# HGRN forget gates and queries by seven products for two heads, with frame operands made once

## The chip, the cores and the metric

The kernel runs on one core of a Trainium2 chip. The metric is the device time of one execution in microseconds (us); a profiled execution also records every engine's instructions, and its span is the time from the first to the last of them.

## What is computed

One layer of a streaming encoder on x of 512 frames by 1024 channels, all in float32. One input projection gives eight parts: zu and zv for a gMLP branch, zq, zf, zi and zo for an HGRN2 recurrence with 8 heads of 128 channels, and two merge gates.

```python
h = rmsnorm(x, norm_mix[l])
proj = h @ w_in[l]
zu, zv, zq, zf, zi, zo, g_a, g_b = jnp.split(proj, split_points, axis=-1)
y_a = gmlp_branch(zu, zv, gmlp_ln_g[l], gmlp_ln_b[l], gmlp_ws[l], gmlp_bs[l]) @ w_up_a[l]
y_b = hgrn2_branch(zq, zf, zi, zo, lower_bounds[l], l, hg_norm_g[l]) @ w_up_b[l]
mix = jax.nn.sigmoid(g_a) * y_a + jax.nn.sigmoid(g_b) * y_b
x = x + mix @ w_out[l]
h = rmsnorm(x, norm_ffn[l])
x = x + jnp.square(jax.nn.relu(h @ w_ff1[l])) @ w_ff2[l]
```

In the recurrence the forget gate is sigmoid(zf), the key k = sigmoid(-zf), the query q = silu(zq); per head S_t = diag(f_t) S_(t-1) + k_t v_t^T and o_t = S_t^T q_t. Each head's o is normalised and gated with silu(zo).

## The kernel before

Every product of float32 matrices is made of reduced-precision matmuls: `split` (L97 to L99) makes a high part H by a copy on ACT (L98) and a low part L by a subtraction on DVE (L99), and `mm3` (L122 to L124) issues three matmuls, H·H, H·L and L·H, for each block of 128 input channels. Weights come in tiles of 128 x 1024 (512 KB) by `wraw` on the queue of SP (L94), four raw tiles in flight; `operand` splits them into WH and WL, of which there are five. `hTH` and `hTL` hold the normalised frames, channels on partitions.

There are two ways to project. `chan_proj` multiplies one weight tile with all 512 frames: 8 blocks x 3 = 24 matmuls of 512 columns for 128 channels. `seven` computes two such tiles at once in a Strassen-Winograd form: the weights of two tiles A and B are seen as 2 x 2 blocks (two groups of 128 channels, two halves of the input channels), the frames as 2 x 2 blocks (two halves of the input channels, two halves of the frames), and seven block products of 12 matmuls of 256 columns replace eight. The sums of weight blocks (s1 to s4) are made on DVE (L147, L148, L154, L155) before they are split; the sums of frame blocks (t1, t2, t4) are made and split once by `frames_operands`.

The stages in order: the norm of x and its transposition; zv and zu with the gMLP branch, whose result y is split into `yaH` and `yaL` group by group (L367); four rounds of the recurrence; the output gate zo (L556 to L559); the projection upa of the gMLP branch (L571); the merge gates GA and GB by `seven`, with `frames_operands` just ahead of them (L593); upb, the output projection, and the two products of the feed-forward part (FFN), of which the first uses four plain tiles and then `seven` with its own frame operands (L675). The last 24 tiles of the FFN's second product add weight tiles with accumulating transfers on the queue of POOL (L760).

A round takes two heads. `proj_round` makes V for both, then for each head forget gate F and key K out of one `chan_proj`, and query Q out of another (Q is gated on DVE, L405). `hgrn_head` has many small matmuls: cell products `sp` of 32 to 96 columns (L417), each followed by masks and decay products on DVE that change K and Q in place; at the end the transposes `pk` of K, the states `pst`, and the output `po` (L534, L536), which is squared on ACT (L538), turned into a factor on POOL (L216, L218) and scaled into `o_n` on DVE (L541).

The program is written stage by stage. A scheduler with a timeline simulation (`schedule_with_timeline_sim=True`) sets the order of the instructions on each engine, so that the projections of the next round lie between the heads of this one; each engine then runs its list in order.

Of the kernel before, what the change touches and what calls it, by code (L numbers as in the profile page):

```python
# [75 lines left out]
def trunk_kernel(ctx: ExitStack, tc: tile.TileContext, A: dict, out: bass.AP):  # L76
# [91 lines left out]
    def frames_operands(pool, H, L, tmp):
# [12 lines left out]
        t1, t2, t3, t4 = x["11"], x["22"], x["12"], x["21"]
        nc.vector.tensor_tensor(t1, x["12"], x["11"], ALU.subtract)
        split(t1, *out["t1"])
        nc.vector.tensor_tensor(t3, x["22"], x["12"], ALU.subtract)
        nc.vector.tensor_tensor(t2, x["22"], t1, ALU.subtract)
        split(t2, *out["t2"])
        split(t3, *out["t3"])
        nc.vector.tensor_tensor(t4, x["21"], t2, ALU.subtract)
        split(t4, *out["t4"])
# [720 lines left out]
```

## Time and profile before

| what | value |
|---|---|
| median of 3 runs | 835.21 us (834.03 to 835.6) |
| profiled execution | 836.09 us, its span 834.2 us |
| mean granted TensorE clock | 0.993 |
| PE busy | 818.7 us, 98%, 6226 instructions |
| PEld (weight loads, beside PE) | 730.5 us, 88% |
| DVE busy | 599.2 us, 72% |
| ACT busy | 408.5 us, 49% |
| POOL busy | 47.1 us, 6% |

Shares are of the span. Matmuls overlap each other, so the time between the starts of two neighbours, and not the listed duration, is what one costs. The granted clock is a share of 2.4 GHz.

### The profile page before, as it was taken

The numbers are of one execution on the slowest core, as the hardware profiler recorded it, in microseconds if no ns is written. First come the engines' busy times: TensorE is split into PE (matmuls) and PEld (weight loads), VectorE is DVE, ScalarE is ACT, GpSimd is POOL, SyncE is SP. The second block draws the span as 40 slices with busy tenths as digits, with TensorE's granted clock in tenths as the row PEclk, the third lists the DMA queues.
The fourth block names the chain that finished last, engine by engine and source line by source line (L and its number), as shares of the span: only waits on it lengthen the run. The fifth ranks groups of instructions, "written<-read, shape, count | busy, mean of one in ns | idle before, by whom it ended". The sixth has DMA issues, their size and how long they took to land.

```text
span 834.2 us, 15111 instructions
## 1 busy us (share of the span) xinstructions
PE 818.7 (98%) x6226; PEld 730.5 (88%) x6226; DVE 599.2 (72%) x955; ACT 408.5 (49%) x676; POOL 47.1 (6%) x81
## 2 busy tenths in 40 slices
PE   8999999999999999999999999899999999999996
PEld 7989888879789988999878889899999988878884
DVE  7563767676685587887574369777777575899996
ACT  6433434344333345556442343677677652555454
POOL 2000000000000000000000021000000000010103
PEclk9999999999999999999999999899999999999998
DMA  9233321221311212323434411233333396193802
GB/s 337 88 110 106 98 67 68 73 66 40 102 52 52 93 36 76 102 101 103 152 101 173 156 62 41 77 105 120 105 103 101 104 303 176 43 292 99 235 11 101
DMA packets 26919, 92.44 MB, mean 111 GB/s; under 512 B 3489, under 2 KB 3873, under 8 KB 26850
## 3 DMA queue, kind: packets, MB, share of 16 engines
q1 hardware_dynamic: 24546, 84.13, 30.4%
q0 software_dynamic: 1728, 6.29, 4.1%
q8 instruction: 49, 0.80, 0.4%
q10 hardware_dynamic: 576, 1.05, 0.3%
q14 instruction: 20, 0.16, 0.1%
HBM read 89.36 MB, written 2.10 MB: 110 GB/s over the span
## 4 chain that ended last, share of the span: by engine, by line
PE 94%; DVE 2%; ACT 1%; issue 1%; POOL 1%; POOLq 0%; ACTq 0%; DVEq 0%
PE acc L122 15%; PE acc L124 15%; PE acc L123 15%; PE prodx L124 5%; PE prodx L122 5%; PE prodx L123 5%; PE prodzy L123 4%; PE prodzy L124 4%; PE prodzy L122 4%; PE hm L122 3%; PE hm L124 3%; PE hm L123 3%; PE y L122 2%; PE y L124 2%; PE y L123 2%; PE sp L417 2%
## 5 line engine op out<-in xcount | busy, mean ns | idle before, releaser
L99 DVE TENSOR_TENSOR WL<-raw,WH 128x1024 fp32r<-128x1024 f32 (+1 forms) x134 | 151.4, 1134 | 101.4 <-ACT WH L98 100.5
L98 ACT ACTIVATE WH<-raw 128x1024 fp32r<-128x1024 f32 (+1 forms) x134 | 132.2, 989 | 164.6 <-PE acc L123 62.7
L122 PE MATMUL acc<-WH,hTH 128*128 128x256 f32 x320 | 91.5, 286 | 0.0
L124 PE MATMUL acc<-WH,hTL 128*128 128x256 f32 x320 | 91.3, 285 | 0.0
L123 PE MATMUL acc<-WL,hTH 128*128 128x256 f32 x320 | 91.0, 284 | 0.0
L122 PE MATMUL acc<-hTH,WH 128*128 128x512 f32 x160 | 64.2, 401 | 0.0
L124 PE MATMUL acc<-hTH,WL 128*128 128x512 f32 x160 | 64.2, 401 | 0.0
L123 PE MATMUL acc<-hTL,WH 128*128 128x512 f32 x160 | 63.5, 397 | 0.0
L99 DVE TENSOR_TENSOR WL<-s,WH 128x1024 fp32r<-128x1024 f32 x44 | 53.8, 1222 | 10.0 <-ACT WH L98 9.0
L122 PEld LDWEIGHTS acc<-WH,hTH 128*128 128x128 f32 x320 | 60.3, 189 | 0.6
L123 PEld LDWEIGHTS acc<-WL,hTH 128*128 128x128 f32 x320 | 60.3, 188 | 0.5
L124 PEld LDWEIGHTS acc<-WH,hTL 128*128 128x128 f32 x320 | 60.3, 189 | 0.2
L98 ACT ACTIVATE WH<-s 128x1024 fp32r<-128x1024 f32 x44 | 46.7, 1062 | 16.1 <-PE prodx L123 9.5
L123 PE MATMUL hm<-WL,aH 128*128 128x512 f32 x96 | 38.0, 396 | 0.0
L124 PE MATMUL hm<-WH,aL 128*128 128x512 f32 x96 | 38.0, 395 | 0.0
L122 PE MATMUL hm<-WH,aH 128*128 128x512 f32 x96 | 37.9, 396 | 0.0
L124 PEld LDWEIGHTS acc<-hTH,WL 128*128 128x128 f32 x160 | 30.0, 188 | 7.1
L123 PEld LDWEIGHTS acc<-hTL,WH 128*128 128x128 f32 x160 | 30.0, 188 | 6.6
L122 PEld LDWEIGHTS acc<-hTH,WH 128*128 128x128 f32 x160 | 30.0, 188 | 6.5
L98 ACT ACTIVATE WH<-rawx 128x1024 fp32r<-128x1024 f32 x24 | 25.1, 1054 | 19.6 <-issue 10.7
L122 PE MATMUL prodx<-h2H,WH 128*128 128x256 f32 x112 | 31.4, 280 | 1.8 <-ACT WH L98 1.8
L123 PE MATMUL prodzy<-h2L,WH 128*128 128x256 f32 x112 | 32.1, 287 | 0.0
(295 smaller groups left out, 2344.6 us busy)
## 6 DMA issues: line engine op xcount, KB each, us to landing
raw<-in_w_dram SPq DMA_DIRECT2D x128, 512.0 KB, 3.6
rawx<-in_w_dram SPq DMA_DIRECT2D x18, 512.0 KB, 8.5
rawx<-in_w_dram POOLq DMA_DIRECT2D x6, 512.0 KB, 6.6
raw<-in_w_dram POOLq DMA_DIRECT2D x6, 512.0 KB, 8.1
x_t<-in_x_dram SPq DMA_DIRECT2D x4, 512.0 KB, 5.7
x<-in_x_dram SPq DMA_DIRECT2D x4, 512.0 KB, 5.2
out_dram<-x ACTq DMA_DIRECT2D x4, 256.0 KB, 2.8
out_dram<-x SPq DMA_DIRECT2D x4, 256.0 KB, 2.4
```

What stands on the lines that cost most here:

```text
L98: nc.scalar.activation(H, src, AF.Copy)
L99: nc.vector.tensor_tensor(L, src, H.bitcast(F32), ALU.subtract)
L122: nc.tensor.matmul(acc, ah, bh, start=first and i == 0, stop=False, **kw)
L123: nc.tensor.matmul(acc, ah, bl, start=False, stop=False, **kw)
L124: nc.tensor.matmul(acc, al, bh, start=False, stop=last and i == n - 1, **kw)
L417: nc.tensor.matmul(sp[p * C:(p + 1) * C, t * n:(t + 1) * n], K[:, t * P + p * C:t * P + (p + 1) * C], x(t, p), start=True, stop=True)
```

## The change

The forget gates and keys of both heads of a round now come from one call of `seven`, the queries from another. In these calls (`dma=True`) the two sums s1 = B1 + B2 and s3 = B1 + A1 are made by transfers: SP loads one summand plain from DRAM (256 KB), and an accumulating transfer on POOL's queue adds the other (256 KB); DVE makes s2 and s4. The signs of three products are turned, so that each sum is an addition, and the callback `fin` applies the sign in the activation that follows. The product x lies in the PSUM tag "acc", and there is one tile zy in place of two.

The frame operands are made once, before the loop over zu, in space of `o_n` that is not used yet, and serve the rounds and the merge gates. y of the gMLP branch stays unsplit (`ya`) and is split in two pieces just before upa. The cell products have two banks in place of four, QX two buffers in place of three; the first cell product of a head moves into the bank of the next. The number of matmuls of the other stages is as before.

The diff, cut to its core:

```diff
-        for h in (2 * r, 2 * r + 1):
-            names += [("chan", ZF + 128 * h), ("chan", ZQ + 128 * h)]
+        names += [("chan", z + 128 * h) for z in (ZF, ZQ) for h in (2 * r, 2 * r + 1)]
...
-    def seven(nameA, nameB, rhs, pool, psum, g, func):
+    def seven(nameA, nameB, rhs, pool, psum, g, fin, dma=False):
...
-        x = ps.tile([P, S], F32, tag="hm", bufs=2, name="prodx")[:, :256]
-        zy = psum.tile([P, 2, S], F32, tag="zy", bufs=2, name="prodzy")
+        xtag = "acc" if dma else "hm"
+        x = ps.tile([P, S], F32, tag=xtag, bufs=2, name="prodx")[:, :256]
+        zy = psum.tile([P, 2, S], F32, tag="zy", bufs=1 if dma else 2, name="prodzy")
...
+        if dma:
+            A1, B = A["w"][index[nameA]][:, :S], A["w"][index[nameB]]
+            for s, more in ((s1, B[:, S:]), (s3, A1)):
+                nc.sync.dma_start(s, B[:, :S])
+                nc.gpsimd.dma_start(s, more, accum_op=ALU.add)
...
-        nc.vector.tensor_tensor(s1, a21, a22, ALU.add)
-        nc.vector.tensor_tensor(s2, s1, a11, ALU.subtract)
+        if not dma:
+            nc.vector.tensor_tensor(s1, a21, a22, ALU.add)
+        nc.vector.tensor_tensor(s2, s1, a11, ALU.add)
         WS = operand(s12)
-        product(y, WS, 0, "t1", True, False)
+        product(y, WS, 0, "n1", True, False)
...
-        nc.vector.tensor_tensor(s3, a11, a21, ALU.subtract)
-        nc.vector.tensor_tensor(s4, a12, s2, ALU.subtract)
+        if not dma:
+            nc.vector.tensor_tensor(s3, a11, a21, ALU.add)
+        nc.vector.tensor_tensor(s4, a12, s2, ALU.add)
...
-        nc.scalar.activation(g[:, 1, 256:], g[:, 1, 256:], func)
+        fin(1, slice(256, S), g[:, 1, 256:])
...
-        nc.scalar.activation(g[:, 0, :], g[:, 0, :], func)
-        product(x, operand(a22), 0, "t4", False, True)
-        nc.scalar.activation(g[:, 1, :256], x, func)
-
-    def frames_operands(pool, H, L, tmp):
+        fin(0, slice(0, S), g[:, 0, :])
+        product(x, operand(a22), 0, "n4", False, True)
+        fin(1, slice(0, 256), x)
+
+    def act_by_sign(g, func):
+        def fin(i, cols, src):
+            nc.scalar.activation(g[:, i, cols], src, func, scale=-1.0 if i else 1.0)
...
+    def frames_operands(pool, H, L, tmp, own3=False, have=()):
         q = {f"{j + 1}{l + 1}": (H[:, 4 * j:4 * j + 4, 256 * l:256 * l + 256],
              for j in range(2) for l in range(2)}
         x = dict(zip(q, tmp))
         for n in ("11", "21", "12", "22"):
-            nc.vector.tensor_tensor(x[n], q[n][0].bitcast(F32), q[n][1].bitcast(F32), ALU.add)
+            if n not in have:
...
+        n2, n4, n1, n3 = x["11"], x["21"], x["12"], x["22"]
+        nc.vector.tensor_tensor(n3, x["22"], x["12"], ALU.subtract)
+        if own3:
+            split(n3, *out["n3"])
+        nc.vector.tensor_tensor(n1, x["11"], x["12"], ALU.subtract)
+        split(n1, *out["n1"])
+        nc.vector.scalar_tensor_tensor(n2, n3, -1.0, x["11"], ALU.mult, ALU.subtract)
+        split(n2, *out["n2"])
+        if not own3:
+            split(n3, *out["n3"])
+        nc.vector.scalar_tensor_tensor(n4, x["21"], -1.0, n2, ALU.mult, ALU.subtract)
+        split(n4, *out["n4"])
...
+    hT = o_n.rearrange("p t d -> p (t d)").rearrange("p (k s) -> p k s", k=KD)
+    hq = [hT[:, 4 * j:4 * j + 4, 256 * l:256 * l + 256] for j in range(2) for l in range(2)]
...
-    yaH = pya.tile([P, NG, S], F32R, name="yaH")
-    yaL = pya.tile([P, NG, S], F32R, name="yaL")
-    shift(pya)
+    ya = pya.tile([P, NG, S], F32, name="ya")
...
+            if t >= 2:
+                nc.scalar.copy(hT[:, 4 * half:4 * half + 4, t * P:(t + 1) * P], pt)
...
+    rhs = frames_operands(ph, hTH, hTL, hq, True, ("12", "22"))
...
-        y = gp.tile([P, S], F32, tag="y", bufs=2, name="y")
-        nc.vector.tensor_tensor(y, m.rearrange("p n q -> p (n q)"), u, ALU.mult)
-        split(y, yaH[:, g, :], yaL[:, g, :])
+        nc.vector.tensor_tensor(ya[:, g, :], m.rearrange("p n q -> p (n q)"), u, ALU.mult)
...
-        heads = []
-        for h in (2 * r, 2 * r + 1):
-            zf = chan_proj(ZF + 128 * h)
-            F = hg.tile([P, S], F32, tag="F", bufs=3, name=f"F{h}")
-            K = hg.tile([P, S], F32, tag="K", bufs=3, name=f"K{h}")
-            nc.scalar.activation(F, zf, AF.Sigmoid)
-            nc.scalar.activation(K, zf, AF.Sigmoid, scale=-1.0)
-            zq = chan_proj(ZQ + 128 * h)
-            Q = hg.tile([P, S], F32, tag="Q1", bufs=2, name=f"Q1_{h}")
-            sq = hg.tile([P, S], F32, tag="sq", bufs=2, name=f"sq{h}")
-            nc.scalar.activation(sq, zq, AF.Sigmoid)
-            nc.vector.tensor_tensor(Q, zq, sq, ALU.mult)
-            heads.append((h, F, K, Q))
-        return V, heads
+        F, K, Q = (hg.tile([P, 2, S], F32, tag=n, bufs=2, name=f"{n}{r}") for n in "FKQ")
+
+        def fin_f(i, cols, src):
+            nc.scalar.activation(K[:, i, cols], src, AF.Sigmoid, scale=1.0 if i else -1.0)
+            nc.scalar.activation(F[:, i, cols], src, AF.Sigmoid, scale=-1.0 if i else 1.0)
+
+        def fin_q(i, cols, src):
+            sq = hg.tile([P, S], F32, tag="sq", bufs=1, name="sq")[:, cols]
+            nc.scalar.activation(sq, src, AF.Sigmoid, scale=-1.0 if i else 1.0)
+            nc.vector.scalar_tensor_tensor(Q[:, i, cols], src, -1.0 if i else 1.0, sq, ALU.mult, ALU.mult)
+
+        for z, g, fin in ((ZF, F, fin_f), (ZQ, Q, fin_q)):
+            seven(("chan", z + 256 * r), ("chan", z + 256 * r + 128), rhs, hg, ps_sc, g, fin, True)
+        return V, [(2 * r + i, F[:, i, :], K[:, i, :], Q[:, i, :]) for i in range(2)]
...
-            return ps_sc.tile([P, S], F32, tag="sp", bufs=4, name=f"sp{h}_{name}")
-
-
-        sp = bank(0)
-        cellwise(sp, lambda t, p: Q[:, t * P + p * C:t * P + (p + 1) * C], C)
-        QX = hg.tile([P, 7 * S // 4], F32, tag="QX", bufs=3, name=f"QX1_{h}").rearrange("p (g x b) -> p g x b", x=7, b=1)
+            return ps_sc.tile([P, S], F32, tag="sp", bufs=2, name=f"sp{h}_{name}")
...
+        QX = hg.tile([P, 7 * S // 4], F32, tag="QX", bufs=2, name=f"QX1_{h}").rearrange("p (g x b) -> p g x b", x=7, b=1)
...
+            if lv == 0:
+
+                cellwise(sp, lambda t, p: Q[:, t * P + p * C:t * P + (p + 1) * C], C, 1, 48 * NT)
...
+    left2 = ExitStack()
+    pu = left2.enter_context(tc.tile_pool(name="pu", bufs=1, side="left", reuse_waits="tile"))
+    yaH = pu.tile([P, NG, S], F32R, name="yaH")
+    yaL = pu.tile([P, NG, S], F32R, name="yaL")
+    for g in range(0, NG, 2):
+        split(ya[:, g:g + 2, :], yaH[:, g:g + 2, :], yaL[:, g:g + 2, :])
...
-    rhs = frames_operands(pt, hTH, hTL, [part[1][:, 2 * i:2 * i + 2, :].rearrange("p d (l t) -> p (d l) t", l=2)
-                                         for i in range(4)])
...
+            seven(("chan", c0 + 128 * d), ("chan", c0 + 128 * d + 128), rhs, pt, ps_g, g, act_by_sign(g, AF.Sigmoid))
...
+        seven(("ff1", f), ("ff1", f + 1), rhs, pq, ps_f, g, act_by_sign(g, AF.Relu))
...
+    nc = _bacc.Bacc("TRN2", target_bir_lowering=False, num_devices=1, dynamic_dma_scratch_size=4096)
```

Three places show how the order on the engines moves. First PE at the end of the last round: `po` is the output of head 7, `acc<-WH,hTH` and its like are products of the output gate, `acc<-yaH,WH` is upa, `py` are transposes of `o_n`. Before:

```order
L122 MATMUL acc<-WH,hTH 128x256
L123 MATMUL acc<-WL,hTH 128x256
L124 MATMUL acc<-WH,hTL 128x256
L534 MATMUL po_3091<-V_2510,scores_694 128x128
L536 MATMUL po_3091<-st_3087,Q_7_3011 128x128
L122 MATMUL acc<-WH,hTH 128x256
L123 MATMUL acc<-WL,hTH 128x256
```

After those rows 37 more products of the output gate follow, and then upa. Now:

```order
L123 MATMUL acc<-WH,hTL 128x256
L608 MATMUL py<-ident,o_n 128x128 x4
L554 MATMUL po_3575<-V_2876,scores_706 128x128
L556 MATMUL po_3575<-st_3571,Q_7_3495 128x128
L554 MATMUL po_3575<-V_2876,scores_706 128x128
L556 MATMUL po_3575<-st_3571,Q_7_3495 128x128
L608 MATMUL py<-ident,o_n 128x128 x4
L121 MATMUL acc<-yaH,WH 128x512 x2
L122 MATMUL acc<-yaL,WH 128x512
L123 MATMUL acc<-yaH,WL 128x512
L121 MATMUL acc<-yaH,WH 128x512
L122 MATMUL acc<-yaL,WH 128x512
```

The last two pairs of `po` have moved behind the last product of the output gate, directly ahead of upa. On DVE the work that stands between the last `po` and the split that upa reads is now:

```order
L98 TENSOR_TENSOR WL<-raw_4267,WH 128x1024
L561 TENSOR_SCALAR o_n<-po_3575,rr_h 128x128 x4
L579 TENSOR_TENSOR o_n<-o_n,sg 128x2x256 x2
L155 TENSOR_TENSOR s_4271<-raw_4269 128x512
L98 TENSOR_TENSOR yaL<-ya,yaH 128x1024
L163 TENSOR_TENSOR s_4272<-raw_4267,raw_4269 128x512
L156 TENSOR_TENSOR s_4271<-s_4271,raw_4267 128x512
L98 TENSOR_TENSOR yaL<-ya,yaH 128x1024
```

Before, all four splits into `yaL` stood ahead of the first round. L579 is the gating of `o_n` (L559 before), L155 makes s2 of the first pair of merge gates.

Second, DVE in the first round, at a hand-over of the buffer s0 from one call of `seven` to the next. K0, Q16_0 belong to head 0 at work, F1 to the next round. Before:

```order
L490 TENSOR_TENSOR K0_846<-K0_846,T4_0_1033 128x16x16
L491 TENSOR_TENSOR Q16_0_1027<-Q16_0_1027,T4_0_1033 128x16x16
L498 COPY_PREDICATED cells0_695<-mask16_691,sp0_16_1042 128x4x16
L490 TENSOR_TENSOR K0_846<-K0_846,T16_0_1059 128x8x32
L491 TENSOR_TENSOR Q16_0_1027<-Q16_0_1027,T16_0_1059 128x8x32
L99 TENSOR_TENSOR WL_1525<-raw19_1522,WH_1524 128x1024
L99 TENSOR_TENSOR WL_1911<-raw20_1908,WH_1910 128x1024
L490 TENSOR_TENSOR K0_846<-K0_846,T32_0_1079 128x4x64
L491 TENSOR_TENSOR Q16_0_1027<-Q16_0_1027,T32_0_1079 128x4x64
```

Now:

```order
L518 COPY_PREDICATED cells0_707<-mask16_703,sp0_16_1173 128x4x16
L98 TENSOR_TENSOR WL_1710<-s0_1681,WH_1709 128x1024
L98 TENSOR_TENSOR WL_1753<-s1_1682,WH_1752 128x1024
L171 TENSOR_TENSOR F1_1547<-u_1558,prodzy_1557 128x512
L510 TENSOR_TENSOR K0_827<-K0_827,T16_0_1190 128x8x32
L511 TENSOR_TENSOR Q16_0_1158<-Q16_0_1158,T16_0_1190 128x8x32
L168 TENSOR_TENSOR F1_1547<-prodx_1556,u3_1559 128x256
L484 TENSOR_TENSOR U1_2_1849<-F1_1547 128x128
L485 TENSOR_TENSOR U1_2_1849<-F1_1547,U1_2_1849 128x128
L98 TENSOR_TENSOR WL_1789<-raw19_1679,WH_1788 128x512
L486 TENSOR_TENSOR T1_2_1850<-F1_1547,U1_2_1849 128x128
L156 TENSOR_TENSOR s0_2275<-s0_2275,raw22_2271 128x512
```

The split of s0_1681 gives the buffer free, into which the two transfers for s0_2275 go; the addition at L156 reads it ten instructions later, and the decay products by T32_0 on K0 have moved behind it.

Third, ACT at the start of the FFN, where act_5501 (act_5976 and act_5973 now) hold frame operands and results, and h2H is a frame operand. Before:

```order
L98 ACTIVATE t1H<-act_5504 128x1024
L98 ACTIVATE WH<-s_5760 128x1024
L98 ACTIVATE WH<-s_5761 128x1024
L671 ACTIVATE act_5501<-acc 128x512 x2
L98 ACTIVATE t2H<-act_5504 128x1024
L98 ACTIVATE WH<-raw_5758 128x512
L672 ACTIVATE act_5501<-act_5501 128x512 x2
L98 ACTIVATE h2H<-act_5504 128x4x256
L98 ACTIVATE t4H<-act_5504 128x1024
L98 ACTIVATE WH<-raw_5879 128x1024
```

Now:

```order
L97 ACTIVATE WH<-s_6232 128x1024
L97 ACTIVATE n1H<-act_5976 128x1024
L97 ACTIVATE n2H<-act_5976 128x1024
L97 ACTIVATE WH<-s_6233 128x1024
L696 ACTIVATE act_5973<-acc 128x512 x2
L97 ACTIVATE WH<-raw_6230 128x512
L97 ACTIVATE n4H<-act_5976 128x1024
L697 ACTIVATE act_5973<-act_5973 128x512 x2
L97 ACTIVATE h2H<-act_5976 128x4x256
L97 ACTIVATE WH<-raw_6351 128x1024
```

The split of t2 (n2 now) has moved ahead of the first Relu (L671, L696 now): between that and the copy of the next whole tile (raw_5879, raw_6351 now) four rows stand in place of five.

## Rows read from the trace of the kernel before

**Rows 1.** The page's totals (engine, busy us, share, instructions) and its chain.

```profile
PE 818.7 (98%) x6226; PEld 730.5 (88%) x6226; DVE 599.2 (72%) x955; ACT 408.5 (49%) x676; POOL 47.1 (6%) x81
...
PE 94%; DVE 2%; ACT 1%; issue 1%; POOL 1%; POOLq 0%; ACTq 0%; DVEq 0%
```

**Rows 2.** Windows: stretch, length, busy us (x) of PE, PEld, DVE, ACT, POOL, PEclk, DMA share, GB/s.

```profile
30.00:90.00 60.00, 60.00 (x363) 53.08 (x363) 32.76 (x52) 22.05 (x28) 4.51 (x12) 1.00 0.33 102
144.00:191.00 47.00, 47.00 (x542) 39.89 (x540) 33.09 (x99) 19.10 (x51) 2.89 (x4) 1.00 0.23 69
```

**Rows 3.** Windows at the start of the merge gates and of the FFN.

```profile
324.00:328.00 4.00, 2.27 (x16) 1.91 (x16) 2.76 (x3) 4.00 (x5) 0.00 (x0) 1.00 0.11 20
524.00:527.00 3.00, 0.67 (x3) 0.38 (x3) 3.00 (x5) 3.00 (x6) 0.00 (x0) 0.82 0.54 165
528.00:532.00 4.00, 4.00 (x21) 4.00 (x21) 1.97 (x2) 1.51 (x3) 0.00 (x0) 0.50 0.47 131
```

**Rows 4.** Timeline of PE in a chan_proj: start us, us, engine, line, op.

```profile
180.56 0.40 PE L123 MATMUL acc<-hTL,WH 128*128 128x512 f32 x1
...
183.83 0.40 PE L122 MATMUL acc<-hTH,WH 128*128 128x512 f32 x1
```

**Rows 5.** Timeline of PE in the merge gates.

```profile
350.00 0.28 PE L124 MATMUL prodx<-t2H,WL 128*128 128x256 f32 x1
...
352.94 0.28 PE L124 MATMUL prodx<-hTH,WL 128*128 128x256 f32 x1
```

**Rows 6.** Groups of DVE by line and form: xcount, busy us, mean ns, idle before.

```profile
L99 DVE TENSOR_TENSOR WL<-raw,WH 128x1024 fp32r<-128x1024 f32 x112 | 136.4, 1222 | 101.1 <-ACT WH L98 100.4
...
L148 DVE TENSOR_TENSOR s<-s,raw 128x512 f32<-128x512 f32 x22 | 15.1, 685 | 0.1
...
L159 DVE TENSOR_TENSOR act<-prodx,u 128x256 f32<-128x256 f32 x14 | 5.9, 419 | 1.7 <-PE prodx L124 1.7
...
L405 DVE TENSOR_TENSOR Q<-acc,sq 128x512 f32<-128x512 f32 x8 | 5.5, 684 | 0.0
```

**Rows 7.** Timeline of PE at the start of the FFN's seven products; [idle before <- releaser].

```profile
525.69 0.38 PE L122 MATMUL prodx<-h2H,WH 128*128 128x256 f32 x1 [1.75 <-ACT WH L98]
...
527.30 0.41 PE L123 MATMUL prodx<-t2L,WH 128*128 128x256 f32 x1
...
532.42 0.41 PE L123 MATMUL prodzy<-h2L,WH 128*128 128x256 f32 x1
```

**Rows 8.** Timeline of ACT just before that.

```profile
520.18 1.06 ACT L98 ACTIVATE t2H<-act 128x1024 fp32r<-128x1024 f32 x1
```

**Rows 9.** Timeline of PE, ACT, POOL and DVE at the last head's end.

```profile
293.96 0.39 PE L536 MATMUL po<-st,Q 128*128 128x128 f32 x2
...
294.44 0.28 ACT L538 ACTIVATE hjunk<-po 128x128 f32<-128x128 f32 x1 [0.97 <-PE po L536]
...
295.21 1.04 POOL L218 TENSOR_TENSOR rr_h<-rs_h,neghalf 128x4 f32<-128x4 f32 x1
...
296.28 1.13 DVE L541 TENSOR_SCALAR o_n<-po,rr_h 128x128 f32<-128x128 f32 x4 [2.08 <-POOL rr_h L218]
297.32 0.68 DVE L559 TENSOR_TENSOR o_n<-o_n,sg 128x512 f32<-128x512 f32 x1
```

**Rows 10.** Windows in the FFN's second product, columns as above.

```profile
720.00:756.00 36.00, 36.00 (x156) 28.77 (x155) 36.00 (x36) 18.21 (x18) 3.49 (x4) 1.00 0.72 204
```

**Rows 11.** DMA issues (tile, queue, count, KB each, median us to landing) and those of L760.

```profile
raw<-in_w_dram SPq DMA_DIRECT2D x128, 512.0 KB, 3.6
...
out_dram<-x SPq DMA_DIRECT2D x4, 256.0 KB, 2.4
...
DMA to landing us min/median/max: 5.5/7.7/10.6
```

More of the change, by code (lines that the diff above doesn't have):

```diff
@@ L163, in seven @@
                                 u.rearrange("p (l t) -> p l t", l=2), zy[:, :, :256], ALU.add)
-        nc.scalar.activation(g[:, 0, :], g[:, 0, :], func)
-        product(x, operand(a22), 0, "t4", False, True)
-        nc.scalar.activation(g[:, 1, :256], x, func)
-    def frames_operands(pool, H, L, tmp):
+        fin(0, slice(0, S), g[:, 0, :])
[4 more added lines that the diff above has]
+            nc.scalar.activation(g[:, i, cols], src, func, scale=-1.0 if i else 1.0)
+        return fin
+    def frames_operands(pool, H, L, tmp, own3=False, have=()):
         q = {f"{j + 1}{l + 1}": (H[:, 4 * j:4 * j + 4, 256 * l:256 * l + 256],
@@ L175, in frames_operands @@
         for n in ("11", "21", "12", "22"):
-            nc.vector.tensor_tensor(x[n], q[n][0].bitcast(F32), q[n][1].bitcast(F32), ALU.add)
+            if n not in have:
+                nc.vector.tensor_tensor(x[n], q[n][0].bitcast(F32), q[n][1].bitcast(F32), ALU.add)
         out = {n: q[n] for n in ("11", "21", "22")}
-        out["t3"] = q["12"]
-        for n in ("t1", "t2", "t4"):
+        out["n3"] = q["12"]
+        for n in ("n1", "n2", "n4") + (("n3",) if own3 else ()):
             out[n] = tuple(pool.tile([P, 4, 256], F32R, name=f"{n}{p}") for p in "HL")
[L181 to L189, printed above, removed]
+        n2, n4, n1, n3 = x["11"], x["21"], x["12"], x["22"]
[10 more added lines that the diff above has]
+        split(n4, *out["n4"])
         return out
@@ L446, in hgrn_head @@
                 "p g x b -> p g (x b)"), 6 * g * b)
+            if lv == 0:
+                cellwise(sp, lambda t, p: Q[:, t * P + p * C:t * P + (p + 1) * C], C, 1, 48 * NT)
             b4 = 4 * b
             if lv == 0:
-                QN = hg.tile([P, 7 * S // 4], F32, tag="QX", bufs=3, name=f"QX{b4}_{h}").rearrange("p (g x b) -> p g x b", x=7, b=b4)
+                QN = hg.tile([P, 7 * S // 4], F32, tag="QX", bufs=2, name=f"QX{b4}_{h}").rearrange("p (g x b) -> p g x b", x=7, b=b4)
                 qn = QN[:, :, 0:4, :].rearrange("p g i (j b) -> p g i j b", b=b)
@@ L472, in hgrn_head @@
             nc.vector.tensor_tensor(kv[:, :, 2, :], kv[:, :, 2, :], bc(T4[:, :, 3]), ALU.mult)
+            if lv == 0:
+                nc.vector.copy_predicated(cl.rearrange("p t c -> p (t c)"), mask[0], sp[:, 48 * NT:(48 + C) * NT])
             spv = sp[:, :NT * 48].rearrange("p (g x b) -> p g x b", x=6, b=b)
@@ L573, in trunk_kernel @@
     right3.close()
+    left2.close()
     def onto_channels(pool, h):
@@ L597, in trunk_kernel @@
             g = part[1][:, d:d + 2, :] if i else pt.tile([P, 2, S], F32, tag="ga", bufs=2, name="ga")
-            seven(("chan", c0 + 128 * d), ("chan", c0 + 128 * d + 128), rhs, pt, ps_g, g, AF.Sigmoid)
+            seven(("chan", c0 + 128 * d), ("chan", c0 + 128 * d + 128), rhs, pt, ps_g, g, act_by_sign(g, AF.Sigmoid))
             if not i:
@@ L678, in trunk_kernel @@
         g = acts[f // 8][:, f % 8:f % 8 + 2, :]
-        seven(("ff1", f), ("ff1", f + 1), rhs, pq, ps_f, g, AF.Relu)
+        seven(("ff1", f), ("ff1", f + 1), rhs, pq, ps_f, g, act_by_sign(g, AF.Relu))
         nc.scalar.activation(g, g, AF.Square)
```

10 lines of the change are left out of this document (4 added, 6 removed).

## The prediction, made before the changed kernel ran

> **What bounds the kernel now.** First the page's totals and its chain of waits [rows 1]: TensorE (PE) is busy 98% of the span and carries 94% of the chain. So a matmul that goes away shortens the time by its own length, and everything else counts only where PE stands still. Second the windows, read for who is idle in a stretch. In the recurrence rounds, of which 144 to 191 us is one, PE is full and VectorE (DVE) has 33.09 of 47.00 us of work [rows 2]. In 30 to 90 us PE is full and DVE has 32.76 of 60 [rows 2]. Two holes stand out [rows 3]: 4.00 − 2.27 = 1.7 us at 324 to 328, after which the granted clock is still 1.00, and 3.00 − 0.67 = 2.3 us at 524 to 527, after which it is 0.50, that is 1.2 GHz in place of 2.4. Third the timeline of single instructions, for the pace of matmuls and for the chains behind the holes.
>
> The profiled execution took 836.1 us; the sum is made against it. The median of the runs shown is 835.2, 0.9 less, and I take the 0.9 off at the end. A measurement here tells about 0.2% (1.7 us) from no change.
>
> **Term 1, PE columns.** Two heads' gates or queries cost 2 × 24 matmuls of 512 columns now. Fourteen steps of that form take 183.83 − 180.56 = 3.27 us, 0.2336 each [rows 4]: 11.21 us per pair. The seven products are 7 × 12 = 84 matmuls of 256 columns; 25 steps of that form, in the merge gates, take 2.94 us, 0.1176 each [rows 5]: 9.88. Eight pairs save 8 × 1.33: **−10.6**, all on the path. The cell products of a head stay the same in number.
>
> **Term 2, the hole at 324.** It lies where the merge gates begin, with the frame operands made just ahead of them. In the new order these are made some 200 us earlier: **−1.7** (bound 0, if another wait stands behind it). DVE does them (ten passes of 128x1024, 1.22 us each as the other passes of that shape [rows 6], 12 us) between 30 and 90, where it has 27 us free; ScalarE (ACT) is less loaded there than DVE [rows 2]. PE asks for them only with the first round, so I cost them at nothing there; if that cover were gone it would be up to 2 us.
>
> **Term 3, the hole at 524.** PE waits 1.75 us for ACT's copy of a weight tile [rows 7], and then runs 24 steps of 256 columns in 532.42 − 527.30 = 5.12 us, 0.213 each in place of 0.118; of such steps the slow stretch has about 27, so the clock costs 2.6. The rewritten `frames_operands` puts one split of an operand ahead of the first Relu that stood behind it; such a copy is 1.06 us on ACT [rows 8]. PE has the same products to cover the rest, so the hole falls from 2.3 to about 1.3. That is under the 1.7 which left the clock at 1.00 [rows 3], so I let the clock stay up: −1.0 − 2.6 = **−3.6** (bounds: 0 if it stays as it is, −5 if both go).
>
> **Term 4, a new hole before upa.** The order now puts the last head's two closing product pairs behind all products of the output gate, and the split of ya behind that head's normalisation on DVE. In the old order 39 products of the output gate and then those of upa followed the last pair, and yaL was long made. The chain behind the last product, from [rows 9]: PE's product ends at 293.96 + 0.39 = 294.35, the last o_n is written when the next instruction begins, 297.32: 2.97 us over ACT, GpSimd (POOL) and DVE. Then two gatings of o_n at 0.68 [rows 9], an addition of s at 0.685 that stands ahead on DVE, and yaL at 1.22 [rows 6]: 6.24 us. ACT has a copy of 1.06 [rows 8] ahead of the square that starts the chain, partly after the product's end; between 6.2 and 7.3 I take 6.7. PE has two matmuls of 512 columns for that time, 0.47 [rows 4], and four transposes, about as much: **+5.8** idle (bounds 5.3 and 6.4). This hole is longer than the 2.3 that dropped the clock [rows 3], so the same price again: **+2.6** (bound 0).
>
> **Term 5, DVE and the transfers in the rounds.** By the passes of [rows 6] a round's projections cost DVE 4 × 1.222 + 2 × 0.684 = 6.3 us now. After: 6 splits of 1024 (7.3), 2 splits of 512, 4 additions of s and 2 of u + zy (8 × 0.685 = 5.5), 2 of 256 columns (0.84) and the query gating in three pieces (1.5): 15.2. So **8.9 more** on 33.1 is 42.0, in a round that shrinks from 47.0 to 44.4: 95%. Of 720 to 756, DVE is busy 36.00 of 36.00 and PE too [rows 10], so a full DVE alone need not stop PE; I cost the load itself at nothing while it leaves 2 us a round.
>
> What may stop it is a chain. The buffer of s1, s3 comes free when DVE has split the pair before; then SyncE (SP) loads 256 KB plain, POOL adds 256 KB by an accumulating transfer, and DVE's addition of s2 waits for that with its whole queue behind it, the decay products on K for PE's next cell products among it. No row shows either transfer at this size. Plain, 512 KB of weights take 3.6 us and 256 KB of output 2.4 [rows 11]: I take 2.8, nearer the output by size. Accumulating, 512 KB took 5.5 at least, 7.7 in the median, 10.6 at most [rows 11], with full queues; I take the least, less the 1.2 by which the plain loads differ: 4.3 (bounds 2.4, as if plain, and 7.7). The chain is **7.1 us** (bounds 4.8 and 11.3). By the new order, with these rows' durations, DVE has 2.7 and 3.0 us of work between release and addition in the first two hand-overs, where it has idle time, and 6.6, 6.6, 7.0, 4.7 and 6.0 in the other five (in the second of these some 1.7 is a wait for PE). It would wait 0.5 + 0.5 + 0.1 + 2.4 + 1.1 = 4.6 us; as DVE has some 2 us of slack a round I pass **+3** of it to PE. Each further us of chain costs up to 5. POOL's queue is held by the same transfers; its normalisation of a head waits behind them, and only the PSUM tile of that head hangs on it: nothing.
>
> *A page on it.* The Trainium skill, "DMA: Bandwidth & Descriptors", section "Anatomy of one DMA — SWDGE (gpsimd) path", gives about 2.0 us plus bytes over 436 GB/s for a transfer issued by GpSimd; by that, an estimate, 2.6 us for 256 KB and 3.2 for 512 KB, a chain of some 5.4, term 5 at nothing and a sum of −7.5. The accumulating rows, 5.5 us at the least for 512 KB, speak against it here, and the sum goes by the rows.
>
> **Sum:** −10.6 − 1.7 − 3.6 + 5.8 + 2.6 + 3.0 = −4.5: 831.6 for a profiled execution, **830.7** for the median. Low end: −10.6 − 1.7 − 5 + 5.3, no clock loss and no waits in the rounds, −12.0: 823.2, I say 823.0. High end: the first rival, 841.2.
>
> **Rivals.**
> 1. *The accumulating chain is late (slower).* Its place is DVE's addition of s2 in the rounds; at 9.2 us, midway between 7.1 and 11.3, five hand-overs lose 2.1 more each, term 5 is 3 + 10.5 = 13.5 and the sum +6.0: 841.2. It eats the gain from a chain of 8.0 us, and makes the kernel slower by more than 0.2% from 8.3. For it: the median of 7.7 for 512 KB. Against it: those transfers run with queues that 720 to 756 shows at 0.72 busy, the rounds at 0.23 [rows 2, 10].
> 2. *No change.* The 524 hole and its slow stretch stay (term 3 at 0) and the rounds cost 4: +0.1, 835.3. For it: one copy fewer is all that the order changes there.
> 3. *Smooth.* The clock does not fall before upa and DVE never waits, because the chain is no longer than the 4.8 us of the lower bound: −10.1, 825.1. For it: a DVE that is full without harm in [rows 10]. Against it: the least accumulating transfer in [rows 11]. The rule of the Trainium skill's page above gives its half on the rounds.
> 4. *The change does not do what it says:* in a round, with PSUM tiles tighter (two banks of sp in place of four, one zy), the 84 products run no faster than the 48, 0.1334 us each. Then term 1 is nothing: 830.7 + 10.6 = 841.3. The merge gates' even pace [rows 5] speaks against it.
>
> **Chances.** The forecast 0.53, of which 0.50 is faster by over 0.2% and 0.03 within; rival 1 0.19 (0.18 slower, 0.01 within); rival 2 0.13 (0.02, 0.09, 0.02); rival 3 0.12, faster; rival 4 0.03, slower. Together: faster 0.64, same 0.13, slower 0.23. The range 823.0 to 841.2 leaves out about half of rivals 1 and 4, the tails of rival 3 and some of the forecast's own unknowns, below 2 in 10.
>
> **What would show it.** Steps of 0.118 us in the rounds' F and Q products and some 10 us less PE work (term 1); no wait of PE where the gates begin (2); the hole at the first products of the FFN near 1.3 us with a clock of 1.00 behind it (3); PE waiting 5 to 6.5 us for yaL before upa and a granted clock near 0.5 behind it (4); in the rounds DVE over 90% busy and waiting for the transfer into s at its addition, in total under 5 us (5). A DVE wait over 2 us at most hand-overs would be rival 1; PE full in the rounds with a time over 836 would mean that I overlooked a place.

## The result and the profile after

The changed kernel takes 840.33 us in the median (838.06 to 841.37, 5 runs) against 835.41 of the kernel before; the ratio is 1.0058 with a 95% interval of 1.004 to 1.0076. It is slower by 4.9 us where 4.5 us less was forecast. The profiled execution has a span of 839.6 us (834.2 before) and a mean granted clock of 0.987 (0.993).

The totals of the page of the changed kernel, for [rows 1]:

```profile
PE 813.0 (97%) x6514; PEld 740.9 (88%) x6514; DVE 621.3 (74%) x1003; ACT 431.7 (51%) x730; POOL 65.8 (8%) x97
```

PE's work fell by 5.7 us only, and what stands beside its work grew from 834.2 − 818.7 = 15.5 to 839.6 − 813.0 = 26.6 us. The view of PE's waits says where; its columns are the total in us, how often, and the longest:

```profile
PE py L608 <- DVE o_n L561: 3.1, 1, 3.1
PE sp L436 <- DVE K L490: 2.8, 1, 2.8
...
PE prodx L121 <- ACT WH L97: 1.8, 2, 0.9
PE prodx L121 <- DVE F L168: 1.7, 1, 1.7
PE prodx L121 <- ACT u L153: 1.3, 3, 0.7
PE acc L122 <- DVE WL L98: 1.2, 2, 0.7
PE po L554 <- ACT hjunk L558: 1.0, 1, 1.0
PE acc L122 <- DVE yaL L98: 1.0, 1, 1.0
```

Two groups are new: waits of 7.6 us in the rounds (sp, F, WL and others, 90 to 290 us), and 3.1 + 1.0 + 1.0 us just before upa. In the kernel before, PE had no wait in that stretch (columns as in [rows 2]):

```profile
90.00:290.00 200.00, 200.00 (x2327) 174.29 (x2326) 139.78 (x394) 79.37 (x199) 10.59 (x14) 1.00 0.22 70
```

**The rounds.** One hand-over of the buffer for s1 and s2, from the timelines of DVE, SP's queue, POOL and PE:

```profile
101.79 1.22 DVE L98 TENSOR_TENSOR WL<-s,WH 128x1024 fp32r<-128x1024 f32 x1
...
111.26 0.69 DVE L156 TENSOR_TENSOR s<-s,raw 128x512 f32<-128x512 f32 x1 [2.69 <-DMA s<-in_w_dram]
...
114.02 0.38 DVE L490 TENSOR_TENSOR K<-K,F 128x128 f32<-128x128 f32 x1
...
103.04 2.29 SPq L149 DMA_DIRECT2D s<-in_w_dram  x2
...
106.58 0.86 POOL L150 DMA_DIRECT2D s<-in_w_dram  x1 [15.59 <-DVE QX L456]
...
114.54 0.73 PE L436 MATMUL sp<-QX,K 128*32 128x48 f32 x32 [2.77 <-DVE K L490]
```

The split frees the buffer at 101.79 + 1.22 = 103.01. SP starts the plain load at 103.04, POOL the accumulating one at 106.58, and DVE's addition runs at 111.26, after 2.69 us in which DVE did nothing: a chain of 8.25 us. The decay of K comes 2.1 us after that addition ends, and PE waits for it. The seven hand-overs took 7.0, 9.1, 8.3, 7.1, 8.2, 7.8 and 8.1 us, 7.9 in the mean, and DVE waited 1.3, 4.1, 2.7, 1.4, 0.4, 2.7 and 1.6: 14.1 in all. The two transfers as the page and the view of L150 have them (median us to landing; minimum, median, maximum), and DVE's wait:

```profile
s<-in_w_dram SPq DMA_DIRECT2D x16, 256.0 KB, 2.8
s<-in_w_dram POOLq DMA_DIRECT2D x16, 256.0 KB, 4.5
...
DMA to landing us min/median/max: 3.7/4.5/8.1
...
DVE s L156 <- DMA s<-in_w_dram: 14.1, 7, 4.1
```

**The clock.** Windows around the hole in the rounds and behind each of the three holes (in the rounds, before upa, at the FFN's start), columns as in [rows 2]:

```profile
112.00:118.00 6.00, 3.46 (x45) 3.38 (x46) 5.97 (x20) 0.91 (x3) 0.00 (x0) 0.73 0.11 17
...
116.00:118.00 2.00, 2.00 (x11) 2.00 (x11) 2.00 (x7) 0.26 (x1) 0.00 (x0) 0.50 0.30 41
302.50:312.70 10.20, 7.19 (x18) 5.38 (x19) 8.32 (x14) 2.54 (x4) 0.82 (x1) 0.50 0.01 3
534.60:538.00 3.40, 3.40 (x18) 3.40 (x18) 2.51 (x4) 2.11 (x4) 0.00 (x0) 0.50 0.09 30
```

In this execution the clock was 0.50, that is 1.2 GHz, for some microseconds at each of the three. Before upa, on PE:

```profile
300.71 0.49 PE L554 MATMUL po<-V,scores 128*128 128x128 f32 x2 [1.01 <-ACT hjunk L558]
...
304.54 1.11 PE L608 MATMUL py<-ident,o_n 128*128 128x128 f32 x4 [3.12 <-DVE o_n L561]
...
307.48 0.80 PE L122 MATMUL acc<-yaL,WH 128*128 128x512 f32 x1 [0.97 <-DVE yaL L98]
...
312.75 0.39 PE L122 MATMUL acc<-yaL,WH 128*128 128x512 f32 x1
```

Twelve steps from 307.48 take 5.27 us, in place of 12 × 0.2336 = 2.80 [rows 4]: 2.5 lost. At the FFN's start, for [rows 7]:

```profile
533.10 0.39 PE L121 MATMUL prodx<-h2H,WH 128*128 128x256 f32 x1 [0.86 <-ACT WH L97]
...
534.33 0.39 PE L121 MATMUL prodx<-n2H,WH 128*128 128x256 f32 x1 [0.73 <-ACT u L153]
...
534.73 0.41 PE L123 MATMUL prodx<-n2H,WL 128*128 128x256 f32 x1
...
538.09 0.28 PE L121 MATMUL prodzy<-h2H,WH 128*128 128x256 f32 x1
```

The hole is 1.6 us (2.3 before), and 16 steps take 3.36 us in place of 1.88, 1.5 lost (2.6 before).

### The profile page after: what moved, and what is told of

The parts are those of the page before. It is cut to its first block, busy times and chain, and to the rows that moved or that the text cites. A ratio compares the mean times of both kernels' runs of the same rounds, so it can differ in the third digit from the quotient of the medians.

```text
span 839.6 us, 15922 instructions
## 1 busy us (share of the span) xinstructions
PE 813.0 (97%) x6514; PEld 740.9 (88%) x6514; DVE 621.3 (74%) x1003; ACT 431.7 (51%) x730; POOL 65.8 (8%) x97
## 4 chain that ended last, share of the span: by engine, by line
PE 56%; issue 1%; ACT 1%; DVE 1%; POOL 0%; POOLq 0%; ACTq 0%; DVEq 0%
PE prodx L121 5%; PE prodx L123 5%; PE prodx L122 5%; PE acc L122 5%; PE acc L121 5%; PE acc L123 5%; PE prodzy L122 4%; PE prodzy L121 4%; PE prodzy L123 4%; PE hm L122 3%; PE hm L121 3%; PE hm L123 3%; PE y L121 2%; PE y L122 2%; PE y L123 2%
## 5 line engine op out<-in xcount | busy, mean ns | idle before, releaser
L98 DVE TENSOR_TENSOR WL<-s,WH 128x1024 fp32r<-128x1024 f32 x60 | 73.1, 1222 | 20.9 <-ACT WH L97 13.8
L97 ACT ACTIVATE WH<-s 128x1024 fp32r<-128x1024 f32 x60 | 63.7, 1061 | 31.8 <-PE acc L122 7.9
L121 PE MATMUL prodx<-n4H,WH 128*128 128x256 f32 x120 | 34.0, 284 | 2.2 <-DVE F L168 1.7
L122 PE MATMUL prodzy<-hTL,WH 128*128 128x256 f32 x128 | 35.9, 281 | 0.0
L123 PE MATMUL prodzy<-hTH,WL 128*128 128x256 f32 x128 | 35.9, 281 | 0.0
L121 PE MATMUL prodzy<-hTH,WH 128*128 128x256 f32 x128 | 35.9, 281 | 0.0
L121 PE MATMUL prodx<-n2H,WH 128*128 128x256 f32 x120 | 34.3, 286 | 1.3 <-ACT u L153 1.3
L123 PE MATMUL prodx<-n2H,WL 128*128 128x256 f32 x120 | 34.1, 285 | 0.0
L122 PE MATMUL prodx<-n2L,WH 128*128 128x256 f32 x120 | 34.0, 283 | 0.0
L122 PE MATMUL prodx<-n4L,WH 128*128 128x256 f32 x120 | 33.7, 281 | 0.0
```

The lines of the kernel that those rows point to most:

```text
L97: nc.scalar.activation(H, src, AF.Copy)
L98: nc.vector.tensor_tensor(L, src, H.bitcast(F32), ALU.subtract)
L121: nc.tensor.matmul(acc, ah, bh, start=first and i == 0, stop=False, **kw)
L122: nc.tensor.matmul(acc, ah, bl, start=False, stop=False, **kw)
L123: nc.tensor.matmul(acc, al, bh, start=False, stop=last and i == n - 1, **kw)
```

## The experiments

Theory A: the loss is two separate holes, one in the rounds from the chain of transfers into s1, one before upa from the last head's chain; each repaired alone gives back its part. Rival B: the rounds lose because DVE has too much work. Rival C: holes only move.

**e1: the sums s1 and s3 on DVE.**

```diff
-        if dma:
-            A1, B = A["w"][index[nameA]][:, :S], A["w"][index[nameB]]
-            for s, more in ((s1, B[:, S:]), (s3, A1)):
-                nc.sync.dma_start(s, B[:, :S])
-                nc.gpsimd.dma_start(s, more, accum_op=ALU.add)
...
-        if not dma:
+        if True:
             nc.vector.tensor_tensor(s1, a21, a22, ALU.add)
...
-        if not dma:
+        if True:
             nc.vector.tensor_tensor(s3, a11, a21, ALU.add)
```

> The changed kernel (840.3 us) with the sums s1 and s3 of the rounds made by VectorE additions, as in the other calls, and not by the plain and accumulating transfers; PSUM tiles as in the change. Theory A (the transfers' chain is late: VectorE waits 14.1 us for it at its addition in the profile of the change): these waits go, 16 additions of 0.685 us (11.0 us) come, net about -3 on VectorE, 836 to 839 us. Rival B (the rounds lose because VectorE has too much work, and the transfers are no matter): 11 us more work on a full engine, 847 to 851 us.

Measured 834.19 us, ratio to before 1.0001 (0.9988 to 1.0015). The kernel before ran at 833.98 beside it, so kernels of different groups are compared by their ratios: 1.0058 to 1.0001 is 0.57%, 4.8 us less than the change. PE, DVE and the others from 90 to 290 us, first the change, then e1:

```profile
90.00:290.00 200.00, 192.43 (x2560) 182.26 (x2559) 162.09 (x444) 100.32 (x245) 22.70 (x25) 0.99 0.40 107
```

```profile
90.00:290.00 200.00, 196.73 (x2625) 187.67 (x2624) 171.00 (x460) 102.97 (x251) 13.36 (x14) 1.00 0.26 81
```

DVE works 8.9 us more, and PE idles 3.3 us instead of 7.6. Rival B falls: the kernel with more work on DVE is the faster one. Theory A's range, 836 to 839, is a gain of 1.3 to 4.3 us on the change's 840.3; measured are 4.8, a little more. The clock's fall at 114 us went too (1.00 over this stretch).

**e2: the same sums on GpSimd.**

```diff
-            A1, B = A["w"][index[nameA]][:, :S], A["w"][index[nameB]]
-            for s, more in ((s1, B[:, S:]), (s3, A1)):
-                nc.sync.dma_start(s, B[:, :S])
-                nc.gpsimd.dma_start(s, more, accum_op=ALU.add)
+            nc.gpsimd.tensor_tensor(s1, a21, a22, ALU.add)
+            nc.gpsimd.tensor_tensor(s3, a11, a21, ALU.add)
```

> The same sums made by additions of 128x512 on GpSimd, from the raw tiles. No row so far shows how long one takes there. Theory A: if two of them are done within 5 us of the buffer's release, VectorE no longer waits at its addition, and TensorE's waits in the rounds (7.5 us) and the slow stretch after the longest of them (about 1.5 us) go: 831 to 834 us. Rival B (VectorE's own load): no change, 839 to 842 us. A third way: an addition on GpSimd and VectorE's passes hinder each other, VectorE's mean durations in the rounds grow, 843 us or more.

Measured 840.59 us, ratio 1.0076 (1.0059 to 1.0094): no gain. From the view of L147 (durations in ns, minimum, median, maximum), the groups of DVE in the rounds of e2, and two of these additions on the timelines of DVE and POOL:

```profile
L147 POOL TENSOR_TENSOR s<-raw x8: 1274/1296/3126, 47.7 to 195.2; 128x512 f32<-128x512 f32 x8
...
L154 DVE TENSOR_TENSOR s<-s,raw 128x512 f32<-128x512 f32 x6 | 8.4, 1399 | 3.6 <-POOL s L147 3.6
...
106.17 1.76 DVE L154 TENSOR_TENSOR s<-s,raw 128x512 f32<-128x512 f32 x1 [1.14 <-POOL s L147]
106.10 1.29 POOL L148 TENSOR_TENSOR s<-raw,raw 128x512 f32<-128x512 f32 x1
...
147.13 0.68 DVE L154 TENSOR_TENSOR s<-s,raw 128x512 f32<-128x512 f32 x1
147.15 1.79 POOL L148 TENSOR_TENSOR s<-raw,raw 128x512 f32<-128x512 f32 x1
```

DVE still waits 5.0 us for POOL. Its own addition takes 1.74 to 1.77 us instead of 0.685 [rows 6] in the four of these six cases in which POOL's second one is already running; where DVE starts first, as at 147.13, it takes 0.68 and POOL's takes 1.79 instead of 1.29. The 1399 ns are the mean of both kinds. That is the mechanism of the third way, though not its time of 843 us or more. The Trainium skill, "SBUF — State Buffer", section "SBUF: two separate sides", has a rule for it: a GpSimd instruction that reads SBUF and a VectorE instruction with two SBUF inputs exclude each other for their whole length. The two pairs of rows agree with it: the instruction that starts second takes 1.1 and 0.5 us longer, near the 1.29 and 0.68 of the one that started first. GpSimd's range of 1.3 to 3.1 us fits it too. The chain got shorter and the wait at the addition smaller, but from 90 to 290 us PE still stood still for 7.7 us.

**e3: ya split into operand buffers, transposes behind upa.**

```diff
+    yaO = [operand(ya[:, g:g + 2, :].rearrange("p g s -> p (g s)")) for g in (0, 2)]
...
-    for g in range(0, NG, 2):
-        split(ya[:, g:g + 2, :], yaH[:, g:g + 2, :], yaL[:, g:g + 2, :])
...
-        mm3(acc, [(blk(UA, (d % 2) * NG + k), (yaH[:, k, :], yaL[:, k, :])) for k in range(NG)])
+        upa = mm3(acc, [(blk(UA, (d % 2) * NG + k), blk(yaO[k // 2], k % 2, S)) for k in range(NG)])
...
-    yb = [onto_channels(pg, h) for h in range(4)]
+    with tc.issue_after(upa):
+        yb = [onto_channels(pg, h) for h in range(4)]
```

> The changed kernel with the two splits of ya made into two of the five weight operand buffers at the end of the output gate, instead of into space that the rounds' tiles hold until head 7 is done; the first four transposes of o_n are queued behind upa on TensorE. Theory A (the hole before upa, 1.01 + 3.12 + 0.97 = 5.1 us of waits and about 2.8 us of a clock at half speed behind it, comes from the chain behind the last product of head 7): both go, 831 to 834 us. Rival C (the hole only moves, to the copies of upa's results or to the start of the merge gates): 837 to 840 us.

Measured 834.34 us, ratio 1.0001 (0.999 to 1.0013): 4.8 us less than the change, by the ratios. The waits before upa are gone, and the matmuls of upa run at full clock. Some came back behind it: 1.39 us for a copy of an upa result, 1.34 and 1.13 us where the crowded transposes meet the first merge gates. So theory A holds for most of it, and rival C for the 3.9 us of these three waits, of which the change had 1.2 at the gates. The edit also makes the splits earlier in the program, ahead of the new pools, so place in memory and place in the program were changed together.

**e10: the same without queueing the transposes** (the last two added lines of e3's diff left out).

> The change with the splits of ya in operand buffers, and the transposes of o_n left where the scheduler puts them (transfers in the rounds as in the change). Term 4 of the prediction named yaL as what TensorE waits for. If that was all, this kernel is as fast as the one that also queues the transposes behind upa (834.3 us). Theory A': the second transpose stands five matmuls behind the last product of head 7 and needs the PSUM tile that this product fills, free only when o_n is written from it: TensorE still waits 2 to 3 us there, 836 to 839 us.

Measured 833.47 us, ratio 0.998 (0.9966 to 0.9994). On PE:

```profile
306.66 0.66 PE L603 MATMUL py<-ident,o_n 128*128 128x128 f32 x4 [2.19 <-DVE o_n L562]
```

The wait that theory A' foretold is there, 2.2 us, for the PSUM tile that the last product of head 7 fills; from 307.2 to 310.6 us, behind it, the clock was 0.50. The time is not the one it gave, though: e3 has 3.9 us of waits from upa to the gates and no lowered clock there, so the two come out near each other. By the ratios e10 is 0.2% the faster, at the edge of what the intervals tell apart. Both show that the split of ya no longer holds PE.

**e4: three buffers for the sums**, on top of e3, with transfers as in the change. The output gate's `sg`, which shares these buffers, has three as well.

```diff
-        s12, s34 = (wp.tile([P, 1024], F32, tag="S", bufs=2, name=f"s{i}") for i in range(2))
+        s12, s34 = (wp.tile([P, 1024], F32, tag="S", bufs=3, name=f"s{i}") for i in range(2))
...
-        F, K, Q = (hg.tile([P, 2, S], F32, tag=n, bufs=2, name=f"{n}{r}") for n in "FKQ")
+        F, K, Q = (hg.tile([P, 2, S], F32, tag=n, bufs=1 if n == "Q" else 2, name=f"{n}{r}") for n in "FKQ")
```

> The kernel of the run before this one (splits of ya in operand buffers) and besides three buffers in place of two for the pairs s1-s2 and s3-s4, paid for by one buffer in place of two for the queries of a round. Theory A: the transfers into s start a product earlier, VectorE's waits of 14.1 us at the addition fall below 5, and the time falls by another 4 to 8 us against the run before. Rival B (VectorE's load): the same time as the run before, within 1.5 us. The single buffer of the queries may cost a wait of its own, seen at the writing of Q.

Measured 829.85 us, ratio 0.9957 (0.9942 to 0.9971): 0.44%, 3.7 us less than e3. Theory A's 4 to 8 us is missed by a little. In its rounds DVE no longer waits for a transfer into s at all, and PE waits 2.6 us:

```profile
90.00:290.00 200.00, 197.39 (x2624) 187.90 (x2623) 164.35 (x445) 101.12 (x249) 20.68 (x24) 1.00 0.37 103
```

This is the most direct test of the chain: the transfers and DVE's additions are the same, and the release comes earlier. What differs besides is the single buffer of the queries, which shows as a wait of 0.6 us of PE. DVE does wait 6.0 us for raw tiles at the same additions, five times, which theory A did not foresee.

**e5: both repairs**, e1 and e3, with the transposes queued behind the fourth tile of upa.

```diff
-        upa = mm3(acc, [(blk(UA, (d % 2) * NG + k), blk(yaO[k // 2], k % 2, S)) for k in range(NG)])
+        last = mm3(acc, [(blk(UA, (d % 2) * NG + k), blk(yaO[k // 2], k % 2, S)) for k in range(NG)])
         nc.scalar.copy(part[0][:, d, :], acc)
+        if d == 3:
+            upa = last
```

> Both single repairs at once: the sums s1 and s3 of the rounds made on VectorE (alone 834.2 us) and the splits of ya in operand buffers (alone 834.3 us); the four transposes of o_n are queued behind the fourth tile of upa, no longer behind the last. Theory A (two separate losses, each 6 us against the change's 840.3): they add, 826 to 829 us. Rival B (VectorE, now with 11 us more work in the rounds, is the bound and only shifts its waits): 831 to 834 us.

Measured 824.98 us, ratio 0.9883 (0.9865 to 0.9901). This is 1.2%, 9.8 us, below the kernel before and 1.7%, 14.6 us, below the change: more than the two gains of 4.8 us. It also spreads the transposes, which neither single repair did; what that brought by itself was not separated. The waits of 1.3 and 1.1 us at the first merge gates, which e3 had, are gone with the transposes spread out, and no stretch before 810 us has a lowered clock.

**e6: s1 on DVE, s3 by the two transfers**, the rest as in e5. Against the change:

```diff
-            A1, B = A["w"][index[nameA]][:, :S], A["w"][index[nameB]]
-            for s, more in ((s1, B[:, S:]), (s3, A1)):
-                nc.sync.dma_start(s, B[:, :S])
-                nc.gpsimd.dma_start(s, more, accum_op=ALU.add)
+            nc.sync.dma_start(s3, A["w"][index[nameB]][:, :S])
+            nc.gpsimd.dma_start(s3, A["w"][index[nameA]][:, :S], accum_op=ALU.add)
...
-        if not dma:
+        if True:
             nc.vector.tensor_tensor(s1, a21, a22, ALU.add)
```

> As the run before, but only s1 is made on VectorE; s3 is still made by the plain and the accumulating transfer. Theory A (it is the transfer into s1 that VectorE waits for, at its next addition; s3 is read two additions later): no wait of note for s3, and 5.5 us less work on VectorE: 0 to 3 us faster than the run before. Rival D (any accumulating transfer in the chain stalls VectorE): slower than it by 2 to 6 us, with waits at the addition of s4.

Measured 826.05 us, ratio 0.9897 (0.9881 to 0.9913): not to be told from e5. No wait for s3 shows in the view of DVE's waits, so rival D falls; the work saved on DVE brings nothing either. The transfers into s3 by themselves do no harm, so the loss goes with those into s1, or with both pairs on the queues together.

**e7: e5 with late squares at the FFN's start.**

```diff
         nc.scalar.activation(act[f], first[f], AF.Relu)
-        nc.scalar.activation(act[f], act[f], AF.Square)
...
-        nc.scalar.activation(g, g, AF.Square)
+        own = nc.scalar.activation(g, g, AF.Square)
+        if f == NPLAIN:
+            with tc.issue_after(own.ins):
+                for a in act[:NPLAIN]:
+                    nc.scalar.activation(a, a, AF.Square)
```

> As the first run of this group, with the squares of the four plain tiles of the FFN queued on ScalarE behind the first pair of seven products. Term 3 of the prediction let the hole at the FFN's start fall from 2.3 to 1.3 us with the clock up; the profile of the change has 1.6 us and the clock down behind it. Two squares (1.15 us) less ahead of the copy that TensorE waits for: the hole falls to about 0.5 us and the clock stays at 1.00, 1 to 3.6 us faster than the first run. Rival: the copy waits for something else (its raw tile, or VectorE's part), and nothing changes.

Measured 824.67 us, ratio 0.9881 (0.9861 to 0.99): not to be told from e5. Windows over the FFN's start, first e5, then e7:

```profile
516.00:540.00 24.00, 22.40 (x188) 21.99 (x188) 19.85 (x26) 16.81 (x30) 0.00 (x0) 1.00 0.32 100
```

```profile
516.00:540.00 24.00, 23.27 (x198) 23.10 (x197) 20.68 (x27) 17.73 (x32) 0.00 (x0) 1.00 0.36 111
```

The hole falls from 1.6 to 0.7 us, as expected. But in e5 the clock stayed at 1.00 behind a hole as large as the one behind which it fell in the change, so there was nothing to win from the clock, and the 0.9 us of the hole are too small to show.

**e8: e4 with spread transposes and late squares.**

> Three buffers for the sums, made by transfers as in the change, one buffer for the queries, splits of ya in operand buffers (together 829.9 us in the run before this group), with the transposes of o_n behind the fourth tile of upa and the late squares. If the waits at the start of the merge gates (1.0 + 1.3 + 1.0 us) came from the transposes being crowded there, 2 to 3 us go, and 1 to 3 at the FFN's start: 824 to 827 us. If they come from elsewhere: 828 to 830 us.

Measured 826.04 us, ratio 0.9906 (0.9888 to 0.9925), 0.5%, 4.3 us less than e4; the waits of 1.3 and 1.0 us at the merge gates are gone, the one of 1.0 for the copy of an upa result stays. A wait of 2.0 us for a copy of V in the first round is larger than in e4 (1.4), and the clock fell behind it.

**e9: e5 without the seven products in the rounds.**

```diff
-            seven(("chan", z + 256 * r), ("chan", z + 256 * r + 128), rhs, hg, ps_sc, g, fin, True)
+            for i in range(2):
+                fin(i, slice(0, S), chan_proj(z + 256 * r + 128 * i))
```

The sign factors in `fin_f` and `fin_q` are taken out with them.

> The kernel with both repairs (sums on VectorE, splits of ya in operand buffers: 825.0 us) with the seven products of the rounds taken out again: forget gates and queries by 24 matmuls of 512 columns for each head, all else as there (frame operands made early, signs positive). Theory A (term 1 of the prediction): 10.6 us of TensorE's work come back, and the 3 us that TensorE waits in the rounds of the kernel with both repairs (0.5 to 0.7 us each) go: 832 to 834 us, with about 817 us of TensorE busy. Rival: VectorE, relieved of 8.9 us a round, sets free more than that, 828 to 830 us.

Measured 830.17 us, ratio 0.9938 (0.9919 to 0.9957). Against e5 that is 0.55%, 4.6 us more, which is what the seven products with DVE sums are worth; both expectations miss by a little. PE is busy 815.1 us, 8.6 more than e5's 806.5. In the rounds of e9:

```profile
90.00:290.00 200.00, 199.20 (x2325) 174.48 (x2325) 137.82 (x394) 78.63 (x199) 11.55 (x14) 1.00 0.22 65
```

PE idles 0.8 us here, 3.2 in e5, and DVE has 33 us less to do than in e5. e9 is itself 0.6%, 5 us, below the kernel before. What is left of the change in it are the frame operands made early, ya's splits in their new place, the spread transposes and the other numbers of buffers; which of these gives the 5 us was not separated.

## Why the prediction was wrong

**Term 1 (−10.6)** was mis-sized. Added up from each start to the next (waits left out), the 672 products for F and Q take 83.3 us in the rounds of the change, 0.124 each. The 384 matmuls of 512 columns for F and Q of the kernel before take 92.6 on the same count, 0.241 each. The gain is 9.3. The pace of long even stretches [rows 4, 5] leaves out what an interruption by cell products costs, and the seven products have more of them: 41 of the 672 steps take about 0.2 us or more at full clock, 32 of the 384 over 0.3. Here, in the changed kernel:

```profile
119.93 0.28 PE L121 MATMUL prodzy<-hTH,WH 128*128 128x256 f32 x1
120.14 0.45 PE L436 MATMUL sp<-Q,K 128*32 128x16 f32 x32
120.51 0.39 PE L122 MATMUL prodzy<-hTL,WH 128*128 128x256 f32 x1
120.74 0.28 PE L123 MATMUL prodzy<-hTH,WL 128*128 128x256 f32 x1
```

The steps around the cell products are 0.21 and 0.23 instead of 0.118. Rival 4, which needs 0.1334 in the mean, does not hold.

**Term 2 (−1.7)** gave 0.5: at the gates' start PE waits 0.92 us for a weight copy and 0.25 for a copy of u, the other wait that the bound of 0 allowed for.

**Term 3 (−3.6)** gave 1.8: the hole is 1.6, not 1.3, and the step that failed is "I let the clock stay up". In the profiled execution the clock fell; e5 has the same hole and a clock of 1.00 behind it, so the rows did not decide this.

**Term 4 (+5.8 and +2.6)** held in size: 5.1 of waits and 2.5 of slow clock in the twelve steps. The place was right, the waiters were not. PE stood first for a square on ACT ahead of the last product pair (1.01 us), which the forecast did not have, then at the second transpose, whose PSUM tile was still held by the last head (3.12), and only then for yaL (0.97). The chain itself gave 4.1, so that 5.1 lies so near to 5.8 is in part luck.

**Term 5 (+3)** is where the forecast failed. It gave 9.0: 7.6 us of waits in the rounds, and a slow stretch behind the longest: 13 steps from 115.20 to 118.14 us take 2.94 us in place of 13 × 0.1176 = 1.53, 1.4 lost. That is 6.0 of the 9.9 us between the forecast −4.5 and the +5.4 of the two profiles. The transfers were priced about right, 2.8 and 4.5 against 2.8 and 4.3. The step that failed is "It would wait 0.5 + 0.5 + 0.1 + 2.4 + 1.1 = 4.6 us": DVE waited 14.1.

Of the 9.5 us between them, 5.4 (1.3 + 4.1) fell on the first two hand-overs, whose waits the forecast left out because DVE has idle time there. The other five waited 8.7 in place of 4.6: their chains, with the issues between the transfers, took 7.9 in the mean, not 7.1, which is 4.0 in all. The work of DVE between release and addition came out near the forecast, 2.8, 3.0, 6.7, 5.0, 6.7, 4.3 and 6.2 us.

The load was forecast too high. DVE was to be busy 95% of a round with 2 us of slack; from 90 to 290 us it was busy 162.09 of 200 us, 81%. So DVE had slack, and it did not shield PE: after the addition at 111.26 the decay of K stood a few instructions behind the blocked one. Nor do all 7.6 us hang on the transfers. Without DVE's waits for them, e1 and e4 still have 3.3 and 2.6 us of waits in the rounds, for squares on ACT, copies and queries, which the forecast put at nothing.

Sum: −9.3 − 0.5 − 1.8 + 5.1 + 2.5 + 7.6 + 1.4 = +5.0, against 839.6 − 834.2 = 5.4 of span; 0.4 is not accounted for, and 0.7 if three of the 13 slow steps, which are in the 83.3 as well, are counted once.

Rival 1 named the mechanism, and e1, e4 and e6 show it: the late accumulating chain at DVE's addition. By the forecast's prices a chain of 7.9 us makes term 5 7.0 and the sum −0.5, just short of rival 1's 8.0 for no gain. The measured sum lies above that because terms 1 to 3 gave 4.3 less than forecast and term 5 another 2.0; term 4 was 0.8 smaller. The formula of the Trainium skill that was weighed ("DMA: Bandwidth & Descriptors", "Anatomy of one DMA — SWDGE (gpsimd) path") gives, as an estimate, 2.6 us for 256 KB issued by GpSimd. The trace has 3.7 for the accumulating ones at the least and 4.5 in the median, so the measurement speaks against it here.
